# Third down pass of an encoder block: unit 8 in half-size products in three of four column groups, and the sums added to the residual in DRAM

## The chip, the cores and the metric

The kernel runs on one core of a Trainium2 chip. The core has a matrix engine (TensorE, PE in the profile), a vector engine (VectorE, DVE), a scalar engine (ScalarE, ACT), GpSimd (POOL) and SyncE (SP). Here SP only issues DMA transfers, POOL issues most of the others, and all transfers share 16 DMA engines. The metric is the device time of one execution in microseconds (us). The kernel before takes 2464.06 us, the median of three runs (2463.86 to 2465.95).

## The reference

One layer of an encoder block over 512 tokens of 2048 features, in float32. Two attention mixers come first, then a channel mixer (SwiGLU) and a final RMSNorm:

```python
x = x + g1 * (merged @ w_out[l])
h2 = rms_norm(x, norm2_w[l]) * (1.0 + sc2) + sh2
ff = (jax.nn.silu(h2 @ w_ffn_gate[l]) * (h2 @ w_ffn_up[l])) @ w_ffn_down[l]
x = x + g2 * ff
return rms_norm(x, final_w)
```

The change lies in the last product, `@ w_ffn_down`, with 5632 rows summed over, and in the sum `x + g2 * ff`.

## The kernel before

Every float32 operand of a product is split into a high and a low part (`split`, L168 on ScalarE makes the high part, L170 on VectorE the low one), and each product is three matmuls (`mm3`, L188 to L190): high by high, high by low, low by high. The 5632 rows of `w_down` are 11 units of 512 rows (four k-tiles of 128). The output's 2048 columns are worked in four groups of 512, numbered `cc` = 0 to 3.

**Two ways to multiply a unit.** `plain` takes the four k-tiles, the four token tiles and the two column halves as they are: two weight loads of 128x1024 (`wsplit`, tile `raw`), two splits, and 96 matmuls of 256 columns. The other way is Strassen's with Winograd's sums: the unit's 512x512 token block and its 512x512 weight block are cut in quarters, and seven products of half the size take the place of eight. `wforms` makes the weight forms in each group: two loads, four sums (L696 to L699, tiles `ta` and `tb`), one split of 512 and three of 1024. `sforms` makes the token forms of a unit once for all groups, with four sums and four splits, into one of three `slots` (tiles `s0`, `s1`, `s2`). This unit then costs 84 matmuls. The forms of weights go through a ring of five `whl` buffers, the raw loads through one of five `raw` buffers.

**Three passes.** Pass 1 does units 0 and 1 plain. Pass 2 does units 2, 3, 4 with half-size products and unit 5 plain. Pass 3 does units 6 and 7 with half-size products and units 8 and 9 plain; its code is the loop at the end that calls `down_group` for each `cc`. Between the passes a group's sum is kept in DRAM (`accd`). Unit 10 is done last, token tile by token tile, with the final norm. In pass 3 group 0 does its plain units first (`lead`), the others last (the `tail` of `down_group`). So the order on TensorE is 8, 9, 6, 7 | 6, 7, 8, 9 | 6, 7, 8, 9 | 6, 7, 8, 9. After a unit, `down_group` calls `behind(u)`, which is `late(cc)` in this pass, and `pump()`, which lets one piece of background work (`bg`) into the program. The eight sums of a group are added into `acc` on VectorE (L1468 to L1485).

**Where things lie.** The token pairs of plain units 8 and 9 lie in `areas`, tiles `a1` and `a0`. In pass 3 the third slot `s2` is given to other things: `xr` (the residual's column group, and two factors) and `fl` (the token pairs of unit 10).

**The residual.** `x` after the first half lies in DRAM in one tensor `x2d`. In pass 3 `residual_of` loads a column group of it into `xr` (L1569) with the row of `g2` for it (L1570). When the next group has done unit 7, `gated_sum` multiplies `acc` by the factor (L1576) and adds it to the residual (L1577), both on VectorE, and stores that to `x2pd` (L1579). During group 3 `late` loads these sums back (L1557) into places that units 6 and 7 leave.

**What sets the order.** A planner orders the instructions of each engine: of those that are ready by its own times, the one that stands first in the program goes first; some parts are marked as more urgent (`tc.high_priority`) or kept in program order (`behind`, `pin`). On the chip each engine and each DMA queue then takes its instructions strictly in that order.

Of the kernel before, what the change touches and what calls it, by code (L numbers as in the profile page):

```python
# [14 lines left out]
F32 = mybir.dt.float32  # L15
# [5 lines left out]
P = 128  # L21
WARM = 12, 14
D = 2048
# [89 lines left out]
def encoder_block(ctx: ExitStack, tc, xp, xT, c, ada1_w, ada2_w, b_ada, norm1_w, w_in, q_norm_w, k_norm_w, bias,  # L113
# [1050 lines left out]

    x2_d = dram.tile([T, D], F32, name="x2d")
    mod["queue"] = nc.sync
# [18 lines left out]
    def residual(cc, g, ssq, eng, x, keep=None):  # L1185
        cs = slice(cc * 512, (cc + 1) * 512)

        def evac(i, b):
            o = io.tile([P, 512], F32, tag="io", name="ro")
            V.tensor_mul(o, b, g[:, cs])  # L1190
            eng.tensor_add(x(i, cc), x(i, cc), o)
            if ssq:
                square(x(i, cc), ssq[i][:, cc:cc + 1])
            if keep is not None:
                t0 = i // 2 * 256 + i % 2
                nc.sync.dma_start(keep[t0:t0 + 255:2, cs], x(i, cc))
        return evac
# [185 lines left out]

    def sforms(j, u):

        big, low = slots[j]
        e, o = (raw_tile("ffe") for _ in range(2))
        for a, r in enumerate((e, o)):
            nc.gpsimd.dma_start(r, ff_d[u][:, a * 1024:(a + 1) * 1024])
        sa = wq.tile([P, 1024], F32, tag="ta", name="sa", bufs=2)  # L1390
        sb = wq.tile([P, 1024], F32, tag="tb", name="sb", bufs=1)
        a11, a21, a12, a22 = e[:, :512], e[:, 512:], o[:, :512], o[:, 512:]
        V.tensor_add(sa[:, :512], a21, a22)
        V.tensor_sub(sa[:, 512:], sa[:, :512], a11)
        V.tensor_sub(sb[:, :512], a11, a21)
        V.tensor_sub(sb[:, 512:], a12, sa[:, 512:])
        d = {}
        for src, t, at, n, rs in ((o, low, 0, 1024, (2, 4)), (a11, low, 2048, 512, (1,)), (sb, big, 2048, 1024, (7, 3)),
                                  (sa, big, 0, 1024, (5, 6))):
            if src is sa:  # L1400
                yield
            hl = [t[:, at + h * n:at + (h + 1) * n] for h in range(2)]
            split(*hl, src)
            for i, r in enumerate(rs):
                d[r] = tuple(h[:, i * 512:(i + 1) * 512] for h in hl)
        sx[u] = d
        yield
# [109 lines left out]
    f0 = 40  # L1517
    xr = p_e.tile([P, 3072 + 64], F32, tag="s23072", name="xr")
    xo = [xr[:, :2048].rearrange("p (i n) -> p i n", i=NT)]
    fl = p_e.tile([P, 4096 + 64], F32R, tag="s24096", name="fl")  # L1520
    wl = {}
    x2p_d = [dram.tile([P, NT, 512], F32, name=f"x2pd{cc}") for cc in range(3)]
    sq3 = [small.tile([P, 4], F32, tag=f"sq{i}", name=f"sq3{i}", bufs=1) for i in range(NT)]
# [8 lines left out]
    def late(cc):  # L1532
        def behind(u):
            if cc == 0 and u == 8:
                while bg:
                    pump()
            if cc == 1 and u > 7:
                a = u - 8
                xl_pairs.append(ff_pair(10, a, [fl[:, a * 2048 + e * 1024:a * 2048 + (e + 1) * 1024] for e in range(2)],
                                        pin=tc.keep_in_program_order))  # L1540
            if u == 7 and due:
                due.pop()()
            if cc == 3 and u == 6:
# [3 lines left out]
            if cc == 3 and u == 7:  # L1547
                x2.append(p_s.tile([P, NT, 512], F32, tag="s13072", name="xd"))
                gf = p_s.tile([P, 2, D], F32, tag="s14096", name="gf")
                wide2.extend((gf[:, 0], gf[:, 1]))  # L1550
                rows(wide2[0], g2_d)
            if cc == 3 and u == 9:
                for c in range(2):
                    us = [gated_split(k, c, *wtiles()) for k in range(0, 4, 2)]
                    wl[c] = [tuple(t[:, e * 512:(e + 1) * 512] for t in hl) for hl in us for e in range(2)]
                for c in range(3):
                    nc.gpsimd.dma_start(x2[c], x2p_d[c])  # L1557
                nc.scalar.dma_start(wide2[1], final_w.partition_broadcast(P))
# [5 lines left out]

    def factor(cc):
        return xr[:, 2048 + cc % 2 * 512:2560 + cc % 2 * 512]

    def residual_of(cc):
        nc.gpsimd.dma_start(xo[0], x2_d[:, cc * 512:(cc + 1) * 512].rearrange("(i p) d -> p i d", p=P))  # L1569
        nc.gpsimd.dma_start(factor(cc), g2_d[cc].partition_broadcast(P).rearrange("p o d -> p (o d)"))  # L1570

    def gated_sum(cc, acc):
        to = xo[0] if cc < 3 else x2[3]
        for t in range(2):
            ts = slice(2 * t, 2 * t + 2)
            behind(V.tensor_mul(acc[:, ts], acc[:, ts], factor(cc).unsqueeze(1).to_broadcast([P, 2, 512])))  # L1576
            behind(V.tensor_add(to[:, ts], xo[0][:, ts], acc[:, ts]))  # L1577
        if cc < 3:
            nc.gpsimd.dma_start(x2p_d[cc], xo[0])  # L1579
            residual_of(cc + 1)  # L1580

    residual_of(0)
    for cc in range(4):
        acc = acc_tile()
        nc.gpsimd.dma_start(acc, acc_d[cc])
        down_group(cc, (6, 7), cl, acc, late(cc), () if cc else (8, 9), late=cc > 1,
                   after_lead=cc == 1)
# [5 lines left out]
    for cc in range(2, 4):  # L1593
        wt = p_s.tile([P, 4096 + 64], F32R, tag=f"a{3 - cc}", name=f"w{cc}")
        hi, lo = (wt[:, 48 + e * 2048:48 + (e + 1) * 2048] for e in range(2))
# [79 lines left out]
```

## Time and profile before

| | us |
|---|---|
| median of three runs | 2464.06 |
| the profiled execution | 2474.1 |
| its span | 2472.3 |
| TensorE busy | 2435.4 |
| VectorE busy | 2007.5 |
| ScalarE busy | 1069.9 |

The profile is that of one execution. Its span runs from the first to the last instruction. TensorE's matmuls overlap in the records, so the distance between their starts is the measure of its pace. "Idle before, releaser" of a group says how long the engine rested before these instructions, and what ended most of that rest. A tile's name stands without its buffer's number.

### The profile page before, as it was taken

The page shows a single profiled execution, that of the slowest core. Times are in us where ns is not written, and L with a number is a line of the kernel's source. Part 1 is how long each engine was busy: PE and PEld are TensorE (multiplying, and loading weights), DVE is VectorE, ACT ScalarE, POOL GpSimd, SP SyncE. Part 2 cuts the span into 40 slices and gives each one's busy share as a digit, 9 for nine tenths or more (in the row PEclk, how much of TensorE's full clock was granted, in tenths as well). Part 3 has the DMA queues.
Part 4 walks back from the last instruction along what each step waited for, and adds up shares of the span by engine and source line. Part 5 has one row for each costly group of instructions (what it writes and reads, how often), then busy time and mean ns, then how long its engine had stood idle before and what let it go on. Part 6 is the DMA issues. An engine that isn't in the chain of part 4 may idle for free.

```text
span 2472.3 us, 42367 instructions
## 1 busy us (share of the span) xinstructions
PE 2435.4 (99%) x17327; PEld 2280.1 (92%) x17327; DVE 2007.5 (81%) x2704; ACT 1069.9 (43%) x1466; POOL 150.9 (6%) x255
## 2 busy tenths in 40 slices
PE   7999999999999999999999999999999999999998
PEld 6888888999888888888999999999999998999997
DVE  7995778999677678667899989889989885687877
ACT  5223455544344523237744444444444454433333
POOL 0100000000011111111000000000000010000010
PEclk9999999999999999999999999999999999999999
DMA  9874322455766687867444444445454466546563
GB/s 357 285 253 144 104 89 80 142 185 181 252 211 231 204 302 248 296 215 228 137 154 155 145 162 147 135 147 163 129 171 147 128 196 214 188 155 233 189 250 121
DMA packets 213730, 461.77 MB, mean 187 GB/s; under 512 B 15152, under 2 KB 59552, under 8 KB 204832
## 3 DMA queue, kind: packets, MB, share of 16 engines
q1 hardware_dynamic: 174160, 309.76, 38.4%
q0 software_dynamic: 29872, 132.73, 15.8%
q10 hardware_dynamic: 9504, 16.58, 1.9%
q8 instruction: 136, 2.23, 0.4%
q14 instruction: 58, 0.48, 0.1%
HBM read 412.84 MB, written 46.17 MB: 186 GB/s over the span
## 4 chain that ended last, share of the span: by engine, by line
PE 72%; DVE 14%; issue 6%; DMA 4%; ACT 1%; POOL 0%; DVEq 0%; POOLq 0%; ACTq 0%
PE mm L190 15%; PE mm L189 15%; PE mm L188 15%; PE S L188 6%; PE S L189 6%; PE S L190 6%; DVE whl L170 4%; PE Y L188 3%; PE Y L189 2%; PE Y L190 2%; DVE raw L524 2%; DMA raw<-in_w_down 2%; DMA raw<-in_w_up 1%; PE T L886 1%; DVE g_acc L631 1%
## 5 line engine op out<-in xcount | busy, mean ns | idle before, releaser
L168 ACT ACTIVATE whl<-raw 128x1024 fp32r<-128x1024 f32 (+1 forms) x483 | 453.9, 943 | 671.1 <-PE mm L190 288.4
L170 DVE TENSOR_TENSOR whl<-raw,whl 128x1024 fp32r<-128x1024 f32 (+1 forms) x483 | 517.9, 1087 | 126.3 <-ACT whl L168 125.9
L168 ACT ACTIVATE whl<-ta 128x1024 fp32r<-128x1024 f32 x124 | 131.4, 1059 | 181.8 <-PE mm L190 107.6
L168 ACT ACTIVATE whl<-tb 128x1024 fp32r<-128x1024 f32 x124 | 131.4, 1060 | 174.5 <-PE S L190 109.8
L170 DVE TENSOR_TENSOR whl<-ta,whl 128x1024 fp32r<-128x1024 f32 x124 | 151.2, 1220 | 40.7 <-ACT whl L168 40.1
L388 DVE SCALAR_TENSOR_TENSOR acc<-mw,cact,acc 128x1024 f32<-128x1024 f32 x124 | 158.8, 1281 | 18.3 <-DMA mw<-in_ada_w 17.9
L170 DVE TENSOR_TENSOR whl<-tb,whl 128x1024 fp32r<-128x1024 f32 x124 | 150.9, 1217 | 4.6 <-ACT whl L168 4.5
L366 POOL DMA_DIRECT2D mw<-in_ada_w x113 | 60.3, 534 | 1361.5 <-DVE acc L388 946.5
L697 DVE TENSOR_TENSOR ta<-raw,ta 128x512 f32<-128x512 f32 x124 | 85.2, 687 | 69.3 <-DMA raw<-in_w_down 29.7
L696 DVE TENSOR_TENSOR ta<-raw 128x512 f32<-128x512 f32 x124 | 85.3, 688 | 36.7 <-DMA raw<-in_w_down 34.3
L188 PE MATMUL mm<-x56h,whl 128*128 128x256 f32 x336 | 92.5, 275 | 0.4 <-DVE c L784 0.4
L189 PE MATMUL mm<-x56l,whl 128*128 128x256 f32 x336 | 92.4, 275 | 0.0
L190 PE MATMUL mm<-x56h,whl 128*128 128x256 f32 x336 | 92.4, 275 | 0.0
L189 PE MATMUL mm<-whl,s 128*128 128x256 f32 x320 | 88.2, 276 | 1.0 <-DVE whl L170 0.8
L188 PE MATMUL mm<-x3h,whl 128*128 128x256 f32 x320 | 88.1, 275 | 0.0
L188 PE MATMUL mm<-whl,s 128*128 128x256 f32 x320 | 88.1, 275 | 0.0
L189 PE MATMUL mm<-x3l,whl 128*128 128x256 f32 x320 | 88.0, 275 | 0.0
L190 PE MATMUL mm<-x3h,whl 128*128 128x256 f32 x320 | 88.0, 275 | 0.0
L188 PE MATMUL S<-x56h,whl 128*128 128x256 f32 x320 | 88.0, 275 | 0.0
L189 PE MATMUL S<-x56l,whl 128*128 128x256 f32 x320 | 88.0, 275 | 0.0
L190 PE MATMUL S<-x56h,whl 128*128 128x256 f32 x320 | 88.0, 275 | 0.0
L190 PE MATMUL mm<-whl,s 128*128 128x256 f32 x320 | 88.0, 275 | 0.0
(1879 smaller groups left out, 8910.9 us busy)
## 6 DMA issues: line engine op xcount, KB each, us to landing
raw<-in_w_in SPq DMA_DIRECT2D x133, 512.0 KB, 4.6
mw<-in_ada_w POOLq DMA_DIRECT2D x113, 512.0 KB, 4.5
raw<-in_w_gate SPq DMA_DIRECT2D x92, 512.0 KB, 4.6
raw<-in_w_up SPq DMA_DIRECT2D x88, 512.0 KB, 4.6
raw<-in_w_down SPq DMA_DIRECT2D x88, 512.0 KB, 5.4
raw<-in_ada_w POOLq DMA_DIRECT2D x29, 1024.0 KB, 6.6
raw<-in_w_out SPq DMA_DIRECT2D x48, 512.0 KB, 5.5
ffd<-c SPq DMA_DIRECT2D x10, 1024.0 KB, 4.8
```

The lines of the kernel that those rows point to most:

```text
L168: high = pin(S.activation(hi, src, AF.Copy))
L170: latest[:] = [high, pin(eng.tensor_sub(lo, src, hi))]
L188: nc.tensor.matmul(o, lh, rh, start=start, stop=False, **kw)
L189: nc.tensor.matmul(o, lh, rl, start=False, stop=False, **kw)
L190: nc.tensor.matmul(o, ll, rh, start=False, stop=stop, **kw)
L366: mod["queue"].dma_start(w, ada2_w[n * P:(n + 1) * P, :])
L388: behind(V.scalar_tensor_tensor(acc, part, cact[:, k:k + 1], acc, op0=ALU.mult, op1=ALU.add))
L524: V.scalar_tensor_tensor(raw, raw, 1.0, call, op0=ALU.mult, op1=ALU.mult, accum_out=y)
L631: V.tensor_add(acc, acc, b)
L696: V.tensor_sub(t1, b12, b11)
L697: V.tensor_sub(t2_, b22, t1)
L886: nc.tensor.transpose(tp[:, k * P:(k + 1) * P], e[:, k * P:(k + 1) * P], ident)
```

## The change

Unit 8 is plain in group 0 alone. In groups 1, 2 and 3 it is done in half-size products after units 6 and 7, and unit 9 stays plain. The order on TensorE becomes 8, 9, 6, 7 | 6, 7, 8, 9 | 6, 7, 8, 9 | 6, 7, 8, 9, with unit 8 of 84 matmuls behind each bar.

The token forms of unit 8 go into slot `s2`. They are made in group 0 behind units 6 and 7, as background work. Their input and sums have a place of their own, the tile `a1` that unit 8's plain pairs leave (`room`): one load of 1 MB on SP's queue, in place of two `raw` buffers and the `ta` and `tb` buffers.

Since `s2` is taken, `xr` is no more. The gated sum of groups 0 to 2 is added to the residual in DRAM by a transfer that adds (`accum_op`), two for a group, issued on POOL's queue; VectorE's two additions for each of these groups are left out. To that end `x2d` becomes eight tensors, one for each column group and token half. Group 3's residual is loaded into SBUF and added there as before. The factors get two small tiles. The token pairs of unit 10 (`fl`) go to `a1` behind the forms, and are loaded on SP's queue. The last weights of group 2 go to `s2` rather than `a1`.

```diff
-    x2_d = dram.tile([T, D], F32, name="x2d")
+    x2_d = [[dram.tile([256, 512], F32, name=f"x2d{cc}{t}") for t in range(2)] for cc in range(4)]
...
-                t0 = i // 2 * 256 + i % 2
-                nc.sync.dma_start(keep[t0:t0 + 255:2, cs], x(i, cc))
+                nc.sync.dma_start(keep[cc][i // 2][i % 2::2, :], x(i, cc))
...
-    def sforms(j, u):
+    def sforms(j, u, room=None):
...
+        else:
+            e, o, sa, sb = (room[:, n * 1024:(n + 1) * 1024] for n in range(4))
+            nc.sync.dma_start(room[:, :2048], ff_d[u])
+            yield
...
+    x2_of = lambda cc, t: x2_d[cc][t].rearrange("(i p) d -> p i d", p=P)
+
+    def load_x2(to, cc):
+        for t in range(2):
+            nc.gpsimd.dma_start(to[:, 2 * t:2 * t + 2], x2_of(cc, t))
...
+            if cc == 0 and u == 9:
+                forms = sforms(2, 8, p_s.tile([P, 4096 + 64], F32, tag="a1", name="f8"))
+                next(forms)
+                bg.append(forms)
             if cc == 1 and u > 7:
                 a = u - 8
-                xl_pairs.append(ff_pair(10, a, [fl[:, a * 2048 + e * 1024:a * 2048 + (e + 1) * 1024] for e in range(2)],
-                                        pin=tc.keep_in_program_order))
-            if u == 7 and due:
-                due.pop()()
+                if a == 0:
+                    fl.append(p_s.tile([P, 4096 + 64], F32R, tag="a1", name="fl"))
+                xl_pairs.append(ff_pair(10, a, [fl[0][:, a * 2048 + e * 1024:a * 2048 + (e + 1) * 1024] for e in range(2)],
+                                        nc.sync, pin=tc.keep_in_program_order))
...
                 rows(wide2[0], g2_d)
+                load_x2(x2[3], 3)
+            if u == 7 and due:
+                due.pop()()
...
                 for c in range(3):
-                    nc.gpsimd.dma_start(x2[c], x2p_d[c])
+                    load_x2(x2[c], c)
...
-    def residual_of(cc):
-        nc.gpsimd.dma_start(xo[0], x2_d[:, cc * 512:(cc + 1) * 512].rearrange("(i p) d -> p i d", p=P))
-        nc.gpsimd.dma_start(factor(cc), g2_d[cc].partition_broadcast(P).rearrange("p o d -> p (o d)"))
+    def factor_of(cc):
+        f = p_e.tile([P, 512], F32, tag="g2f", name="g2f", bufs=2)
+        nc.gpsimd.dma_start(f, g2_d[cc].partition_broadcast(P).rearrange("p o d -> p (o d)"))
+        factors.append(f)

     def gated_sum(cc, acc):
-        to = xo[0] if cc < 3 else x2[3]
+        f = factors.pop(0).unsqueeze(1).to_broadcast([P, 2, 512])
         for t in range(2):
             ts = slice(2 * t, 2 * t + 2)
-            behind(V.tensor_mul(acc[:, ts], acc[:, ts], factor(cc).unsqueeze(1).to_broadcast([P, 2, 512])))
-            behind(V.tensor_add(to[:, ts], xo[0][:, ts], acc[:, ts]))
+            behind(V.tensor_mul(acc[:, ts], acc[:, ts], f))
+            if cc == 3:
+                behind(V.tensor_add(x2[3][:, ts], x2[3][:, ts], acc[:, ts]))
+            else:
+                nc.gpsimd.dma_start(x2_of(cc, t), acc[:, ts], accum_op=ALU.add)
         if cc < 3:
-            nc.gpsimd.dma_start(x2p_d[cc], xo[0])
-            residual_of(cc + 1)
+            factor_of(cc + 1)
...
-        down_group(cc, (6, 7), cl, acc, late(cc), () if cc else (8, 9), late=cc > 1,
+        down_group(cc, (6, 7, 8) if cc else (6, 7), {9: cl[9]} if cc else cl, acc, late(cc), () if cc else (8, 9), late=cc > 1,
                    after_lead=cc == 1)
...
-        wt = p_s.tile([P, 4096 + 64], F32R, tag=f"a{3 - cc}", name=f"w{cc}")
+        wt = (p_e if cc == 2 else p_s).tile([P, 4096 + 64], F32R, tag="s24096" if cc == 2 else "a0", name=f"w{cc}")
```

More of the change, by code (lines that the diff above doesn't have):

```diff
@@ L1382, in __getitem__ @@
             return tuple(Tokens(half(t)[:, :, q]) for t in self.pairs[j])
-    def sforms(j, u):
+    def sforms(j, u, room=None):
         big, low = slots[j]
[L1387 to L1391, printed above, removed]
+        if room is None:
+            e, o = (raw_tile("ffe") for _ in range(2))
+            for a, r in enumerate((e, o)):
+                nc.gpsimd.dma_start(r, ff_d[u][:, a * 1024:(a + 1) * 1024])
+            sa = wq.tile([P, 1024], F32, tag="ta", name="sa", bufs=2)
+            sb = wq.tile([P, 1024], F32, tag="tb", name="sb", bufs=1)
+        else:
+            e, o, sa, sb = (room[:, n * 1024:(n + 1) * 1024] for n in range(4))
+            nc.sync.dma_start(room[:, :2048], ff_d[u])
+            yield
         a11, a21, a12, a22 = e[:, :512], e[:, 512:], o[:, :512], o[:, 512:]
@@ L1517, in encoder_block @@
     f0 = 40
[L1518 to L1522, printed above, removed]
+    fl, wl = [], {}
+    x2_of = lambda cc, t: x2_d[cc][t].rearrange("(i p) d -> p i d", p=P)
+    def load_x2(to, cc):
+        for t in range(2):
+            nc.gpsimd.dma_start(to[:, 2 * t:2 * t + 2], x2_of(cc, t))
     sq3 = [small.tile([P, 4], F32, tag=f"sq{i}", name=f"sq3{i}", bufs=1) for i in range(NT)]
@@ L1563, in encoder_block @@
     due = []
-    def factor(cc):
-        return xr[:, 2048 + cc % 2 * 512:2560 + cc % 2 * 512]
-    def residual_of(cc):
-        nc.gpsimd.dma_start(xo[0], x2_d[:, cc * 512:(cc + 1) * 512].rearrange("(i p) d -> p i d", p=P))
-        nc.gpsimd.dma_start(factor(cc), g2_d[cc].partition_broadcast(P).rearrange("p o d -> p (o d)"))
+    def factor_of(cc):
+        f = p_e.tile([P, 512], F32, tag="g2f", name="g2f", bufs=2)
+        nc.gpsimd.dma_start(f, g2_d[cc].partition_broadcast(P).rearrange("p o d -> p (o d)"))
+        factors.append(f)
     def gated_sum(cc, acc):
-        to = xo[0] if cc < 3 else x2[3]
+        f = factors.pop(0).unsqueeze(1).to_broadcast([P, 2, 512])
         for t in range(2):
             ts = slice(2 * t, 2 * t + 2)
-            behind(V.tensor_mul(acc[:, ts], acc[:, ts], factor(cc).unsqueeze(1).to_broadcast([P, 2, 512])))
-            behind(V.tensor_add(to[:, ts], xo[0][:, ts], acc[:, ts]))
+            behind(V.tensor_mul(acc[:, ts], acc[:, ts], f))
[3 more added lines that the diff above has]
+                nc.gpsimd.dma_start(x2_of(cc, t), acc[:, ts], accum_op=ALU.add)
         if cc < 3:
-            nc.gpsimd.dma_start(x2p_d[cc], xo[0])
-            residual_of(cc + 1)
-    residual_of(0)
+            factor_of(cc + 1)
+    factors = []
+    factor_of(0)
     for cc in range(4):
```

## The prediction

> **What bounds the kernel now.** I read the page first, for the engine that fills the span.
>
> ```profile
> span 2472.3 us, 42367 instructions
> PE 2435.4 (99%) x17327; PEld 2280.1 (92%) x17327; DVE 2007.5 (81%) x2704; ACT 1069.9 (43%) x1466; POOL 150.9 (6%) x255
> ```
>
> TensorE is busy 99% of the span, VectorE is second. The change sits in the third down pass, so next I read busy time in that pass's four column groups (columns: stretch, length, then busy time and count of PE, PEld, DVE, ACT, POOL, the clock, DMA share, GB/s).
>
> ```profile
> 2258.10:2298.30 40.20, 40.20 (x362) 40.20 (x361) 30.82 (x40) 15.82 (x17) 1.61 (x3) 1.00 0.60 202
> 2298.30:2338.50 40.20, 40.20 (x362) 40.20 (x361) 35.39 (x44) 14.34 (x15) 2.91 (x5) 1.00 0.59 204
> 2338.50:2378.70 40.20, 40.20 (x362) 40.20 (x361) 30.96 (x39) 12.44 (x13) 2.39 (x4) 1.00 0.56 200
> 2378.70:2418.90 40.20, 40.20 (x362) 40.20 (x361) 28.84 (x30) 13.65 (x14) 5.03 (x9) 1.00 0.80 294
> ```
>
> TensorE never rests in these 160.8 us and holds full clock. A group is 360 matmuls by the code (two half-size units of 84, two plain units of 96), so a matmul takes 40.20/360 = 0.1117 us. VectorE is the next limit, 35.4 of 40.2 us in the second group. All that TensorE waits for from 2240 us to the end:
>
> ```profile
> PE S L189 <- DVE whl L170: 1.0, 1, 1.0
> PE mm L189 <- DVE w L170: 0.3, 1, 0.3
> ```
>
> So every matmul removed is worth its full 0.1117 us, as long as VectorE delivers the forms in time. To see how much time it has, I place the units on TensorE's timeline.
>
> ```profile
> 2279.54 0.28 PE L188 MATMUL mm<-whl,s 128*128 128x256 f32 x1
> ...
> 2317.06 0.28 PE L188 MATMUL Y<-whl,a 128*128 128x256 f32 x1
> ...
> 2418.90 0.38 PE L188 MATMUL S<-whl,fl 128*128 128x512 f32 x1
> ```
>
> Group 0's plain units 8 and 9 end at 2279.54, so unit 8 ends 96 × 0.1117 earlier, at 2268.82. Four half-size units follow without a break (6 and 7 of group 0, 6 and 7 of group 1), 9.38 us each, until 2317.06. The last product of group 3 ends at 2418.90.
>
> **The matmuls removed.** A plain unit is 4 k-tiles × 4 token tiles × 2 halves × 3 terms = 96 matmuls; a half-size one is 7 products × 2 × 2 × 3 = 84. Groups 1, 2 and 3 lose 12 each: 36 × 0.1117 = **4.02 us**, the whole gain on the bounding engine, and less than 0.2% of the run (4.93 us), which is about what a measurement of this kernel can tell from no change.
>
> **VectorE's price.** Its queue in the stretch with four units in a row:
>
> ```profile
> 2273.10 0.69 DVE L696 TENSOR_TENSOR ta<-raw 128x512 f32<-128x512 f32 x1 [6.18 <-DMA raw<-in_w_down]
> ...
> 2274.91 0.69 DVE L170 TENSOR_TENSOR whl<-raw,whl 128x512 fp32r<-128x512 f32 x1
> ...
> 2284.25 1.82 DVE L170 TENSOR_TENSOR whl<-raw,whl 128x512 fp32r<-128x512 f32 x2
> ...
> 2289.11 0.69 DVE L697 TENSOR_TENSOR ta<-raw,ta 128x512 f32<-128x512 f32 x1 [1.18 <-DMA raw<-in_w_down]
> ...
> 2301.65 1.21 DVE L170 TENSOR_TENSOR whl<-tb,whl 128x1024 fp32r<-128x1024 f32 x1
> ...
> 2303.39 0.68 DVE L698 TENSOR_TENSOR tb<-raw 128x512 f32<-128x512 f32 x1
> 2303.99 0.68 DVE L699 TENSOR_TENSOR tb<-raw,ta 128x512 f32<-128x512 f32 x1
> 2304.59 1.21 DVE L170 TENSOR_TENSOR whl<-raw,whl 128x1024 fp32r<-128x1024 f32 x1
> 2305.73 1.21 DVE L170 TENSOR_TENSOR whl<-ta,whl 128x1024 fp32r<-128x1024 f32 x1
> 2306.86 1.21 DVE L170 TENSOR_TENSOR whl<-tb,whl 128x1024 fp32r<-128x1024 f32 x1
> 2308.00 1.21 DVE L1576 TENSOR_TENSOR acc<-acc,xr 128x1024 f32<-128x1024 f32 x1
> ```
>
> From start to start, a 512-wide operation takes 0.60 us and a 1024-wide one 1.14. A unit's weight forms are four sums, one short split and three long ones: 4 × 0.60 + 0.60 + 3 × 1.14 = 6.42 us; a plain unit's two splits are 2.28. So each of groups 1 to 3 gains 4.14 us of VectorE work. The token forms of unit 8, made once in group 0, have the same operations: 6.42 us. Against that the three residual sums of groups 0 to 2 go, six of these:
>
> ```profile
> L1577 DVE TENSOR_TENSOR xr<-xr,acc 128x1024 f32<-128x1024 f32 x6 | 7.3, 1222 | 0.1
> ```
>
> Six × 1.14 = 6.84 us. The balance is 3 × 4.14 + 6.42 − 6.84 = +12.0 us. The pass then has 126.0 + 12.0 = 138 us of VectorE work in 156.8 us: it fits on average. Groups 2 and 3 I cost at nothing; what hides them is VectorE's own idle time there (9 and 11 us of each 40.2), against 4.14 − 2.28 = +1.9 us each. ScalarE gains a split and a half per unit and is busy 12 to 16 us of 40.
>
> Groups 0 to 1 are another matter. From 2273.10 to 2308 VectorE rests only 1.18 us, and into this stretch goes all of the 6.42 us: the token forms' load needs the place that unit 8 leaves at 2268.82, and their work is given out behind units 6 and 7 of group 0, ahead of the forms of unit 7 and of group 1. How late are the forms then? Unit 7's first, at 2284.25 + 0.60, is needed at 2279.54 + 9.38 = 2288.92: slack 4.1. The last one of group 1's unit 6 is done at 2301.65 + 1.21 = 2302.86 and needed 60 matmuls after 2298.30, at 2305.00: **slack 2.14 us**, the tightest point I find. After it the slack grows: unit 7's last form is done at 2308.07 and needed 60 matmuls after 2307.68, at 2314.38, 6.3 us later. So 6.42 us put in ahead of the tightest point make TensorE wait 6.42 − 2.14 = **4.28 us**. Then unit 8 of group 1: VectorE reaches it at 2308.0 + 6.42 + 2 × 1.14 (the two products of group 0's sum that stay) = 2316.7, needs 6.42 and is done at 2323.1; TensorE wants the last form at 2317.06 + 4.28 + 6.70 = 2328.0. No second wait.
>
> The bounds of this wait: 0, if the work slips into time that I count as full; 4.28 − 1.14 − 1.18 = 1.96, if the fourth split falls behind the tight point and the one idle gap is used; and above, what a wait costs beyond itself. The only other wait of the down passes shows that, in the second pass's last group, where token forms were also made beside three half-size units:
>
> ```profile
> 2231.30 0.28 PE L190 MATMUL S<-whl,s 128*128 128x256 f32 x1
> 2232.44 0.38 PE L188 MATMUL S<-whl,s 128*128 128x256 f32 x1 [0.87 <-ACT whl L168]
> 2233.70 0.38 PE L189 MATMUL S<-whl,s 128*128 128x256 f32 x1 [0.88 <-DVE whl L170]
> ```
> ```profile
> 2229.00:2240.00 11.00, 9.25 (x66) 8.87 (x65) 9.98 (x13) 6.01 (x7) 1.58 (x3) 0.84 0.82 287
> ```
>
> Two waits, 2.2 us beyond the normal pace, and then a mean clock of 0.84 over 11 us: 0.16 × 11 = 1.76 us more. I take 4.28 and keep 0 and 4.28 + 1.76 = 6.04 for the range. The Trainium skill, "TensorE: Matmul & The Clock Gate", Part 1, says the clock falls only after about 3.4 us of idling; by it the sequel would not come from waits this short, and the upper end would be 4.28. The row speaks against it, and the row decides.
>
> **The other edits.** Ten 1 MB transfers of the residual become six half-size sums in DRAM and eight half-size loads, plus one 1 MB load of unit 8:
>
> ```profile
> xr<-x2d POOLq DMA_DIRECT2D x4, 1024.0 KB, 10.3
> x2pd<-xr POOLq DMA_DIRECT2D x3, 1024.0 KB, 5.2
> xa<-x2pd POOLq DMA_DIRECT2D x2, 1024.0 KB, 7.4
> xb<-x2pd POOLq DMA_DIRECT2D x1, 1024.0 KB, 9.5
> ```
>
> No row shows a transfer that adds; I bound it by a plain store, 5.2 us, and twice the slowest row, 20.6. Group 2's sum is issued about 2390 and its columns are read after 2418.90: even 20.6 + 10.3 us of transfer and reload are nearly covered, so 0, nearest to the store. On POOL's queue the reloads, and the next group's accumulator load, stand behind the sums; the accumulator is wanted again only a group later, after 40 us. The token pairs of unit 10 move from POOL's queue to SP's, the last weights of group 2 into another tile, the factors into two small ones: covered the same way, 0 each (a lost cover would cost at most one landing, 5 to 10 us). In the last stretch,
>
> ```profile
> 2405.22 1.23 DVE L1528 TENSOR_TENSOR raw<-raw,gf 128x1024 f32<-128x1024 f32 x1 [3.25 <-DMA gf<-g2d]
> ```
>
> the gate row arrives 2405.22, freed by unit 7 of group 3. The end of the pass comes 1.34 us sooner after that unit than before, so between −1.3 us (its present waits gone) and +1.34 (as much later). I take 0.
>
> **Sum:** −4.02 + 4.28 = +0.26 us on the profiled execution's 2474.1 (span 2472.3 and 1.8 around it), 2474.4. That execution is 10.0 us over the median of the runs; the difference carries over unchanged: 2464.06 + 0.26 = **2464.3**.
>
> **Rivals.** *The forms are hidden* (no wait): for it, form making elsewhere runs beside full TensorE, and the order on VectorE is a planner's, which may put them elsewhere; against it, the stretch is full. −4.02, with up to 1.34 given back at the end: 2460.0 to 2461.4, middle 2460.7; with the last stretch's waits gone too, 2458.7.
>
> *SP's queue stands* (slower). The load of unit 8 is given out on SP ahead of unit 6's weights and waits for TensorE until 2268.82. Before, SP issued weights at these times:
>
> ```profile
> 2263.42 0.37 SPq L195 DMA_DIRECT2D raw<-in_w_down  x1
> 2266.95 0.37 SPq L195 DMA_DIRECT2D raw<-in_w_down  x1
> ```
>
> If it stands ahead of them, the second goes out at 2269.2, 2.3 us later, behind 1 MB (2.8 us, an estimate: group 3's 294 GB/s at a share of 0.80 make 368 GB/s in full). Queued behind it are all later weights, and VectorE waits for them: it starts 5.1 us later than 2273.10, and the tightest point is 4.28 + 5.1 = 9.4 us late: −4.02 + 9.4 + 1.76 = +7.1, 2471.2. With that sequel it is slower by over 0.2% from 2.9 us of delay upward. Against it: the planner may give the weights out first, as they are ready 1.9 us sooner.
>
> *The change does not get its third group*: unit 8 of group 1 is fed too late and only two groups gain, 2 × 1.34 less the same wait: 2464.06 − 2.68 + 4.28 = 2465.7. The 4.9 us of slack worked out above speak against it.
>
> **Chances.** The wait eats the gain 0.42 (2462.0 to 2466.1), hidden 0.27, SP stands 0.18, third group 0.05, the rest (order elsewhere, the end) 0.08. Faster by over 0.2% needs the hidden case and the last waits gone: 0.10, with 0.03 of the rest, 0.13. Slower: SP 0.18 and 0.04: 0.22. Within: 0.65. The range reaches from just under 2458.7 to just over 2471.2.
>
> **What would show it.** Right: 252 matmuls on forms in groups 1 to 3; VectorE without rest from 2273 to 2323; one or more TensorE waits on forms between 2288 and 2306, about 4 us together; nothing from then to the end of group 3. Hidden: no wait there and 28.1 us per three units in each group. SP: the load of unit 8 issued before the two weights, and VectorE's first sum after 2277. Wrong altogether: a wait that is not on VectorE's forms, or a last stretch over 2 us longer or shorter.

## The result and the profile after

The changed kernel takes 2492.45 us (median of four runs, 2490.23 to 2495.96) against 2465.01 us for the kernel before beside it: 1.0107 times as long, with a 95% interval from 1.0095 to 1.0119. That is 27.4 us slower (23 to 29). The prediction said 2464.3 us with a range to just over 2471.2, so it failed, and with it every rival that it had priced.

The page of the changed kernel begins (busy time, share and count of each engine):

```profile
span 2489.2 us, 42338 instructions
PE 2433.5 (98%) x17291; PEld 2277.1 (91%) x17291; DVE 2018.4 (81%) x2724; ACT 1077.5 (43%) x1476; POOL 157.0 (6%) x257
```

TensorE has 36 matmuls less, and VectorE has 10.9 us more, about the 12.0 that were worked out. So the changed work is what was foreseen, and the time lies in waits. All waits of TensorE from 2240 us on (waiter, releaser, us in total, times, longest):

```profile
PE Y L189 <- DVE whl L170: 11.2, 1, 11.2
PE mm L189 <- DVE whl L170: 2.9, 3, 1.8
PE mm L188 <- ACT w L168: 2.8, 1, 2.8
PE S L189 <- DVE whl L170: 2.8, 3, 1.7
PE Y L188 <- DVE acc L1489: 1.9, 1, 1.9
PE mm L189 <- DVE w L170: 1.8, 1, 1.8
PE T L189 <- DVE whl L170: 1.5, 1, 1.5
```

Before there were two, 1.3 us in all. To place them, the pass is cut at the first matmul of each run of units. These are busy times by stretch (same columns as in the prediction): the five half-size units of groups 0 and 1; group 1's unit 9; group 2's half-size units and its unit 9; the same two for group 3; unit 10 as the last stretch.

```profile
2270.89:2323.47 52.58, 47.96 (x423) 47.20 (x421) 45.52 (x57) 25.15 (x28) 3.07 (x3) 1.00 0.46 124
2323.47:2334.19 10.72, 10.72 (x99) 10.72 (x97) 9.77 (x14) 3.08 (x3) 0.57 (x1) 1.00 0.90 329
2334.19:2364.11 29.92, 28.93 (x254) 28.36 (x253) 22.97 (x30) 11.84 (x13) 3.05 (x3) 1.00 0.53 133
2364.11:2375.09 10.98, 10.98 (x98) 10.79 (x97) 6.48 (x10) 2.13 (x2) 0.58 (x1) 1.00 0.65 240
2375.09:2405.39 30.30, 28.41 (x254) 28.21 (x253) 20.74 (x26) 10.18 (x11) 3.91 (x4) 1.00 0.67 189
2405.39:2429.02 23.63, 12.42 (x98) 12.23 (x97) 11.47 (x14) 4.01 (x4) 6.49 (x10) 0.78 0.73 248
2429.02:2479.53 50.51, 44.13 (x206) 37.59 (x204) 43.19 (x71) 16.09 (x39) 0.00 (x0) 0.97 0.24 84
```

Before, the last stretch read:

```profile
2418.90:2462.48 43.58, 42.23 (x206) 36.51 (x204) 38.50 (x67) 15.13 (x37) 0.00 (x0) 1.00 0.23 83
```

At full pace 420 half-size matmuls take 46.9 us, 252 take 28.14 and 96 take 10.72. So groups 0 and 1 lose 5.7 us, group 2 loses 1.8 + 0.3, group 3's half-size units 2.2, its unit 9 12.9, and the last stretch 6.9 over before. Together that is 29.8, less the 4.0 of the matmuls: 25.8 us, within the interval of the measured difference. The two spans differ by 16.9 us only, since the profiled execution of before was itself 10 us over its median: its group 0 begins unit 6 at 2279.54, 8.65 us later than here, so most of that lies ahead of these stretches. Stage by stage the two can be compared.

The largest loss begins on POOL's queue in group 3. After:

```profile
2387.23 0.72 POOL L1527 DMA_DIRECT2D xa<-x2d  x1 [22.50 <-PE mm L190]
2389.80 1.22 POOL L1591 DMA_DIRECT2D x2d<-acc  x1 [1.86 <-DVE acc L1587]
2396.93 1.22 POOL L1591 DMA_DIRECT2D x2d<-acc  x1 [5.91 <-issue]
2397.66 1.25 POOL L1527 DMA_DIRECT2D xa<-x2d  x1
2405.57 1.46 POOL L1527 DMA_DIRECT2D xa<-x2d  x2 [6.67 <-issue]
2407.01 1.65 POOL L439 DMA_DIRECT2D gf<-g2d  x3
```

Before:

```profile
2396.69 1.60 POOL L439 DMA_DIRECT2D gf<-g2d  x3 [2.52 <-PE S L190]
```

The first load of the gate row (`gf`, L439) goes out 2407.01 − 2375.09 = 31.9 us after group 3's start; before it was 2396.69 − 2378.70 = 18.0 us. Ahead of it stand the two adding transfers and the reloads, and POOL stands 5.91 and 6.67 us for which the view names no releaser. The landing times in the trace do: the two adding transfers landed at 2396.61 and 2405.26 (6.8 and 8.3 us after they went out), and each time POOL went on 0.3 us later, at 2396.93 and 2405.57. So POOL stood each time until the adding transfer before had landed. What waits for the row is VectorE:

```profile
2394.68 1.23 DVE L170 TENSOR_TENSOR whl<-tb,whl 128x1024 fp32r<-128x1024 f32 x1
2413.86 1.23 DVE L1534 TENSOR_TENSOR raw<-raw,gf 128x1024 f32<-128x1024 f32 x1 [17.95 <-DMA gf<-g2d]
2415.00 0.68 DVE L1475 TENSOR_TENSOR acc<-acc,p 128x512 f32<-128x512 f32 x1
2415.60 2.35 DVE L170 TENSOR_TENSOR whl<-raw,whl 128x1024 fp32r<-128x1024 f32 x2
```

The product of the last unit's weights with the gate row stands in VectorE's order ahead of group 3's sums (L1475) and of the splits for group 3's unit 9 (L170, 2415.60). VectorE rests 17.95 us with all of them behind it, and TensorE waits 11.2 us for those splits. The wait carries the name of VectorE's `whl`, but its cause is a transfer on a queue of another engine.

### The profile page after: what moved, and what is told of

It reads as the page before. It is cut to its first block, busy times and chain, and to the rows that moved or that the text cites. A ratio compares the mean times of both kernels' runs of the same rounds, so it can differ in the third digit from the quotient of the medians.

```text
span 2489.2 us, 42338 instructions
## 1 busy us (share of the span) xinstructions
PE 2433.5 (98%) x17291; PEld 2277.1 (91%) x17291; DVE 2018.4 (81%) x2724; ACT 1077.5 (43%) x1476; POOL 157.0 (6%) x257
## 4 chain that ended last, share of the span: by engine, by line
PE 70%; DVE 15%; DMA 6%; issue 5%; ACT 1%; POOL 0%; DVEq 0%; SPq 0%; POOLq 0%; ACTq 0%
PE mm L190 15%; PE mm L189 15%; PE mm L188 15%; PE S L188 6%; PE S L190 5%; PE S L189 5%; DVE whl L170 4%; DMA raw<-in_w_down 4%; PE Y L188 2%; PE Y L189 2%; PE Y L190 2%; DVE raw L524 2%; PE T L886 1%; DMA ffr<-ffd 1%; DVE acc L1489 1%
## 5 line engine op out<-in xcount | busy, mean ns | idle before, releaser
L170 DVE TENSOR_TENSOR whl<-raw,whl 128x1024 fp32r<-128x1024 f32 (+1 forms) x483 | 515.8, 1083 | 121.8 <-ACT whl L168 121.5
L170 DVE TENSOR_TENSOR whl<-ta,whl 128x1024 fp32r<-128x1024 f32 x127 | 154.8, 1219 | 41.8 <-ACT whl L168 41.8
L170 DVE TENSOR_TENSOR whl<-tb,whl 128x1024 fp32r<-128x1024 f32 x127 | 154.5, 1217 | 3.3 <-ACT whl L168 3.1
L189 PE MATMUL mm<-whl,s 128*128 128x256 f32 x368 | 101.6, 276 | 3.0 <-DVE whl L170 2.9
L188 PE MATMUL mm<-whl,s 128*128 128x256 f32 x368 | 101.3, 275 | 0.0
L190 PE MATMUL mm<-whl,s 128*128 128x256 f32 x368 | 101.2, 275 | 0.0
```

The lines of the kernel that those rows point to most:

```text
L170: latest[:] = [high, pin(eng.tensor_sub(lo, src, hi))]
L188: nc.tensor.matmul(o, lh, rh, start=start, stop=False, **kw)
L189: nc.tensor.matmul(o, lh, rl, start=False, stop=False, **kw)
L190: nc.tensor.matmul(o, ll, rh, start=False, stop=stop, **kw)
```

## The experiments

Each kernel was timed beside the kernel before, and ratios are to that.

**1. The gate row on another queue.**

```diff
-    def rows(dst, src):
+    def rows(dst, src, queue=nc.gpsimd):
...
-                rows(wide2[0], g2_d)
+                rows(wide2[0], g2_d, nc.scalar)
```

> The changed kernel with one edit: the four loads of the gate row for the last stretch are issued on ScalarE's queue instead of POOL's. Theory A (the gate row is late because it stands on POOL's queue behind the adding transfers and the reloads, and VectorE, which waits 17.9 us for it in order, keeps unit 9's weight splits and the sums of group 3 behind it): the row goes out near 2394 instead of 2407, the 11.2 us wait of TensorE in unit 9 of group 3 goes, and most of the 6.9 us by which the last stretch is longer; 2492.5 - 13 to 20 = 2473 to 2480. Rival B (the adding transfers crowd the DMA engines, so that whatever loads then is late): the row lands 7 us or more after its issue plus the delay it has now, less than 3 us gained, 2489 to 2492. Rival C (the half-size unit 8 overloads VectorE, the wait for the row is only where that shows): no gain, 2490 to 2493.

Measured: 2476.41 us, ratio 1.0043 (1.0028 to 1.0059), 16 us less than the change (1.0107 to 1.0043 of 2465 us). In its trace the row goes out 19.7 us after group 3's start (2393.23, group 3 from 2373.57), VectorE's rest for it shrinks to 4.46 us, and group 3's unit 9 runs at full pace:

```profile
2393.23 2.13 ACTq L439 DMA_DIRECT2D gf<-g2d  x4
2398.74 2.36 DVE L1534 TENSOR_TENSOR raw<-raw,gf 128x1024 f32<-128x1024 f32 x2 [4.46 <-DMA gf<-g2d]
```

So the queue behind which the row stood is shown as the largest cause. ScalarE's queue does not owe this to a faster transfer: counted from group 3's start the row's first part landed 13.7 us sooner than in the change, 12.3 of them since it went out sooner and 1.4 since it took 5.4 us from issue to landing in place of 6.8. In the stages, 12.9 of the 16 us are those that group 3's unit 9 lost. The waits in groups 0 and 1, the 1.8 us in group 3 and a last stretch of 50.7 us stay.

**2. Plain stores in place of adding ones.** The products of groups 0 to 2 are stored plainly into tensors of their own and reloaded from there; the residual of these groups is left out.

```diff
-                nc.gpsimd.dma_start(x2_of(cc, t), acc[:, ts], accum_op=ALU.add)
+                nc.gpsimd.dma_start(x2s_of(cc, t), acc[:, ts])
...
```

> The changed kernel, but the six adding transfers are plain stores of the gated product to DRAM tensors of the same shape, and the reloads read these (so the residual of groups 0 to 2 is left out of the sum). Theory A, if POOL's standing of 5 to 7 us after each adding transfer is a property of adding: the second of a pair and all behind it go out some 6 us earlier, the gate row lands 6 to 9 us earlier, 2492.5 - 6 to 9 = 2483 to 2487. If the standing comes from the number of descriptors on POOL's queue, which is the same here: no change, 2490 to 2493. Rival B: most of the 20 us come back, 2472 to 2478. Rival C: no change.

Measured: 2485.62 us, ratio 1.008 (1.0062 to 1.0097), 6.7 us less than the change.

```profile
2392.23 0.73 POOL L1595 DMA_DIRECT2D x2s<-acc  x1 [0.88 <-DVE acc L1591]
2393.38 0.71 POOL L1595 DMA_DIRECT2D x2s<-acc  x1 [0.41 <-DVE acc L1591]
...
2400.22 0.55 POOL L439 DMA_DIRECT2D gf<-g2d  x1
```

A plain store holds POOL 0.72 us, an adding one 1.22, and after a plain one POOL goes on within 0.8 us in place of about 6. The gate row leaves 19.6 us after group 3's start (2380.64), but POOL stands here too, 2.2 to 3.3 us three times among the reloads and the parts of the row. The row's last part is issued as late as 2407.79, and TensorE still waits 3.5 us before unit 9.

**3. Unit 8 plain, the sums in DRAM kept.**

```diff
-        down_group(cc, (6, 7, 8) if cc else (6, 7), {9: cl[9]} if cc else cl, acc, ...
+        down_group(cc, (6, 7), cl, acc, ...
...
```

> The changed kernel with unit 8 plain in all four groups, as before, and no token forms of it; sums into DRAM, factors, reloads and their queues stay. Theory A: TensorE gets 4.0 us of matmuls more, the 5.7 us of waits in groups 0 and 1 go, and the last part stays late, since the gate row still stands behind the sums and reloads: 2492.5 + 4.0 - 5.7 - 0 to 6 = 2485 to 2491. Rival C: the time of the kernel before comes back, 2463 to 2467. Rival B: 2488 to 2491.

Measured: 2484.97 us, ratio 1.0075 (1.0057 to 1.0093). Without any change to the products the kernel is still 18 us slower. All four groups are at full pace; the row leaves at 2409.20 and the loss of this pass lies in the last stretch (from 2418.99), whose first 24 matmuls take 18.4 us, with these waits:

```profile
PE S L189 <- DVE whl L170: 9.6, 4, 5.4
```

The stretch takes 56.1 us against 43.6 before. That is 12.6 of the 18 us; the rest is not placed, since this profiled execution, like that of before, was already late when group 0 began unit 6 (2279.63).

**4. The token forms put off by one step of the background work.**

```diff
-                bg.append(forms)
+                bg.append(itertools.chain([None], forms))
```

> The changed kernel with the token forms of unit 8 given out one unit later: their sums and three splits behind unit 7 of group 0 instead of unit 6, the last split behind unit 6 of group 1. The theory of the record (VectorE's 6.42 us of forms are too much in groups 0 and 1, wherever they stand): the waits there stay at 4 to 6 us, 2490 to 2494. The other reading of the new trace (VectorE stands 5.3 us in order for the load of unit 8, with unit 6's last weight form behind it; the work itself would nearly fit): the waits in groups 0 and 1 fall from 5.7 to 1 to 3 us, 2487 to 2491. The last part stays late by either.

Measured: 2491.88 us, ratio 1.0104 (1.0082 to 1.0126). The planner gave out the forms at nearly the same place (groups 0 and 1 take 52.2 us in place of 52.6), so the edit did not do what it was meant to, and it tells nothing of the forms. The next two hold them back by a dependency instead, and both have the gate row on ScalarE's queue.

**5. The forms held behind group 0's unit 7.** Their sums and splits may go out only after the last weight form of that unit.

```diff
-                bg.append(forms)
+                bg.append(itertools.chain([None] * 1, forms))
...
+        held = [] if room is None else latest[:]
+        with tc.issue_after(held[1].ins) if held else contextlib.nullcontext():
             V.tensor_add(sa[:, :512], a21, a22)
...
+            hold[:] = held
             split(*hl, src)
+            hold.clear()
...
```

> The gate row on ScalarE's queue (as in the run before, 2476.4), and the token forms of unit 8 held, on VectorE and ScalarE, behind the last weight form of group 0's unit 7. They still stand ahead of the tightest point of the record (the last form of group 1's unit 6), but nothing urgent stands behind VectorE's wait for their load any more. The theory of the record (6.42 us of work against 2.14 us of slack): 4.3 us of waits in groups 0 and 1, against 6.4 in the run before, 2474 to 2475. The reading that VectorE's standing for the load makes the wait: 0 to 1.5 us of waits, 2470 to 2472.

Measured: 2475.77 us, ratio 1.0038 (1.0024 to 1.0051). In the change VectorE rests 5.33 us for the forms' load with unit 6's last weight form behind it:

```profile
2275.15 0.69 DVE L1397 TENSOR_TENSOR f<-f 128x512 f32<-128x512 f32 x1 [5.33 <-DMA f<-ffd]
...
2278.10 1.22 DVE L170 TENSOR_TENSOR whl<-tb,whl 128x1024 fp32r<-128x1024 f32 x1
```

Here that rest is gone, and yet groups 0 and 1 take 52.31 us, 5.4 over full pace; the four waits have become one, at the start of group 1's unit 6:

```profile
PE mm L189 <- DVE whl L170: 3.5, 1, 3.5
```

Behind that wait the granted clock reads 0.50 (2296.00 to 2299.30); 3.4 us at half clock are another 1.7 us, so that wait and clock make 5.2 of the 5.4. So the rest for the load is not the cause by itself: the forms are 6.4 us of work ahead of a point that leaves less than that.

**6. The forms held behind group 1's unit 6.** The same with `[None] * 2`.

> As the one with the forms behind unit 7 of group 0, but held behind the last weight form of group 1's unit 6, which is the tightest point: all of the work then comes after it, where the record finds 6.3 us of slack growing. By the record: 0 to 2.7 us of waits (the forms of unit 8's weights come late by that if the gated products go first), 2470 to 2473. If it is the mere amount of VectorE work between 2262 and 2317 that counts, wherever it stands: 4 us or more, 2474 to 2476.

Measured: 2472.23 us (ten runs), ratio 1.0029 (1.0017 to 1.0041). Groups 0 and 1, then groups 1 (unit 9) and 2, then group 3, then the last stretch:

```profile
2271.52:2320.02 48.50, 47.60 (x422) 47.12 (x421) 46.41 (x59) 24.24 (x27) 3.07 (x3) 1.00 0.51 139
2320.02:2369.60 49.58, 49.58 (x446) 49.58 (x445) 42.14 (x56) 17.25 (x18) 4.19 (x5) 1.00 0.67 206
2369.60:2408.46 38.86, 38.86 (x350) 38.86 (x349) 33.10 (x38) 14.47 (x15) 6.97 (x9) 1.00 0.83 263
2408.46:2458.13 49.67, 43.92 (x206) 37.47 (x204) 38.73 (x67) 16.25 (x38) 1.24 (x2) 0.97 0.31 113
```

The tight point is passed, groups 2 and 3 have no wait at all (38.86 us is 28.14 + 10.72), and 1.6 us are left in groups 0 and 1, where VectorE is busy 46.41 of 48.50 us: this is what the added work costs when its place is good. The 1.8 to 1.9 us wait in group 3 went too, though nothing there was changed; why is not settled. The last stretch is still 49.67. Its longest wait, with what leads to it:

```profile
2421.61 1.22 DVE L1538 TENSOR_TENSOR raw<-raw,gf 128x1024 f32<-128x1024 f32 x1
2422.86 1.06 ACT L168 ACTIVATE w<-raw 128x1024 fp32r<-128x1024 f32 x1 [6.95 <-DVE raw L1538]
2423.97 0.80 PE L188 MATMUL mm<-w,fl 128*128 128x512 f32 x1 [3.15 <-ACT w L168]
```

TensorE waits for ScalarE's split, and that for a gate product on VectorE, which works without rest from 2411.26 until then, on group 3's sums among other things.

**7. The gate row taken out of the weights altogether.** Experiment 1, and all columns are multiplied by the row when they are taken from PSUM, where the matmuls leave their sums; before, only column group 2 was.

```diff
-        if cc != 2:
+        if False:
             V.tensor_mul(r3, r3, wide2[0]...
...
-        if cc == 2:
+        if True:
             g = io.tile(...
```

> The gate row on ScalarE's queue, and the weights of the last unit are not multiplied by the gate row beforehand (six 1024-wide products of VectorE); instead every column's sum is multiplied when it is taken from PSUM, as group 2's already is (12 more 512-wide products, spread over the last stretch). What is left of the loss at the end (7.1 us of waits on the weights of the last unit, after the gate row comes in time). If VectorE's pile causes it (sums of group 3, splits and products all after the gate row, 30 us of work from 2398 on): 6.8 us less of it, 4 to 6 us gained, 2470 to 2472. If the full DMA engines cause it (share 1.0 from 2390 to 2420): the weights come no sooner, 0 to 1.5 us, 2475 to 2477.

Measured: 2479.74 us, ratio 1.0059 (1.0036 to 1.0082), not the 2470 to 2472 that the theory gave. Last stretch on TensorE, and what follows its last matmuls:

```profile
2415.18:2457.77 42.59, 42.23 (x206) 36.43 (x204) 38.78 (x69) 15.20 (x34) 2.15 (x3) 1.00 0.33 115
2457.77:2473.80 16.03, 0.00 (x0) 0.00 (x0) 10.06 (x26) 3.39 (x10) 0.00 (x0) 0.65 0.37 131
```

TensorE's waits in the last stretch are gone but for 0.3 us, so it was VectorE's pile of work (sums of group 3, gate products, splits) that held it. With the products went VectorE's rest for the row, 4.46 us in experiment 1; the two were not separated here, but experiment 10 keeps that rest. But VectorE now ends late: 10.06 us of its work in 16.03 us stand behind the last matmul; in the change the same tail is 9.67 us. The work was moved to a worse place.

**8. Unit 8 plain and the gate row on ScalarE's queue** (the edits of 1 and 3).

> Unit 8 plain in all groups, sums into DRAM as in the change, gate row on ScalarE's queue. If the 7.1 us at the end and the waits in groups 0 to 3 come from the half-size unit 8 (its forms, and a tail of one plain unit where there were two, to hide group 3's VectorE work under): the time of the kernel before, 2463 to 2467. If the adding transfers and reloads by themselves cost something besides the gate row (full DMA engines): 2469 to 2473.

Measured: 2466.39 us, ratio 1.0006 (0.9996 to 1.0017): the time of before. From group 0's unit 6 to the end of group 3, and the last stretch:

```profile
2274.02:2413.38 139.36, 139.36 (x1251) 139.36 (x1249) 108.42 (x130) 49.71 (x52) 14.08 (x16) 1.00 0.63 193
2413.38:2455.08 41.70, 41.69 (x206) 36.67 (x204) 34.78 (x63) 14.13 (x36) 1.42 (x2) 1.00 0.33 115
```

Adding in DRAM costs nothing that can be told from noise once nothing urgent stands behind it on the queue: here too the second adding transfer of group 2 goes out 8.3 us after the first (2383.99 and 2392.28), and TensorE waits for nothing from 2240 us on. All that is left in experiment 1 comes with the half-size unit 8. With the change and experiments 1 and 3 this makes a square: taking the row off POOL's queue gains 0.64% with unit 8 half-size and 0.69% with it plain, so the two losses stand beside each other.

**9. A tail of two plain units in group 3 again.** Experiment 6, but group 3 does unit 8 plain, its token pairs loaded and split anew into `s2`.

```diff
-        down_group(cc, (6, 7, 8) if cc else (6, 7), {9: cl[9]} if cc else cl, acc, ...
+        down_group(cc, (6, 7, 8) if cc in (1, 2) else (6, 7),
+                   {8: again, 9: cl[9]} if cc == 3 else {9: cl[9]} if cc else cl, acc, ...
...
+            if cc == 2 and u == 8:
+                f8 = p_e.tile([P, 4096 + 64], F32R, tag="s24096", name="f8p")
+                for a in range(2):
+                    again[a] = ff_pair(8, a, [f8[:, a * 2048 + e * 1024:a * 2048 + (e + 1) * 1024] for e in range(2)],
+                                       nc.sync, pin=tc.keep_in_program_order)
...
```

> The forms held back and the gate row on ScalarE's queue as in the last run of that kind (2472.2 us), and now unit 8 is half-size in groups 1 and 2 only. In group 3 it is plain again, with its token pairs loaded and split anew into slot s2 during group 3. Group 3 so gets back the 12 matmuls (+1.34 us) and a tail of two plain units, 21.44 us on TensorE in place of 10.72. Theory A (the last stretch is late because a tail of one unit is too short to hide the end-of-group sums, the splits and the gate products): the last stretch falls from 49.7 us to 42 to 44.5, and the time is 2472.2 + 1.3 - (5.2 to 7.7) = 2465.8 to 2468.3. Theory B (it is late for another reason that stays, such as late reloads or the late gate row): the last stretch stays at 48 to 51, and the time is 2472 to 2476. Theory C (the anew loaded token pairs, 2 MB more, get in the way of group 3's weights): waits on forms in group 3 itself, over 2474.

Measured: 2470.04 us, ratio 1.0013 (1.0003 to 1.0022). The last stretch falls from 49.67 to 45.77 us, between the two theories:

```profile
2411.93:2457.70 45.77, 43.61 (x206) 37.84 (x204) 37.30 (x65) 14.25 (x36) 2.15 (x3) 0.96 0.38 134
```

VectorE is no longer late by its work; it rests for weights that arrive late:

```profile
2415.94 1.23 DVE L1538 TENSOR_TENSOR raw<-raw,gf 128x1024 f32<-128x1024 f32 x1 [2.87 <-DMA raw<-in_w_down]
```

So the longer tail does help, by 3.9 us here. What is left over experiment 8's 41.70 is one wait of 2.16 us behind this rest and a low clock after it (last section). The weights may be late because of the 2 MB that this experiment loads anew, which was not tested. A plain unit 8 also needs 4.14 us less of VectorE's time for its weights in group 3, by the prediction's count, so length of tail and amount of work were not separated.

**10. Two column groups multiplied afterwards.** Experiment 6, with the gate row multiplied into the weights of column groups 0 and 1 alone.

```diff
-        if cc != 2:
+        if cc < 2:
             V.tensor_mul(r3, r3, wide2[0]...
...
-        if cc == 2:
+        if cc > 1:
             g = io.tile(...
```

> Forms held back and gate row on ScalarE's queue (2472.2 us), unit 8 half-size in all three groups, and the gate row is multiplied into the weights only for columns groups 0 and 1; columns 2 and 3 are multiplied when taken from PSUM (before: column 2 only). This takes 2 x 1.14 = 2.3 us of VectorE's work out of the pile before the last stretch and puts about 4 x 0.6 us into the last stretch. Theory A (VectorE's pile is the bound of the last stretch): the waits there shrink by 2.3 to 4 us, the last stretch is 45.5 to 47.5 in place of 49.7, the time 2468 to 2470.5. Theory B (ScalarE's splits, held by late weights, are the bound): unchanged within 1.5 us, 2471 to 2473.5.

Measured: 2468.02 us (ten runs) beside 2466.32, ratio 1.0000 (0.9989 to 1.0011).

```profile
2408.72:2452.46 43.74, 42.42 (x206) 36.54 (x204) 37.07 (x66) 15.99 (x36) 1.16 (x2) 1.00 0.36 131
2452.46:2464.10 11.64, 0.00 (x0) 0.00 (x0) 6.00 (x19) 2.67 (x8) 0.00 (x0) 0.72 0.26 90
```

Taking 2.3 us of VectorE's work away ahead of the last stretch shortens it by 5.9 us, 49.67 to 43.74, more than the 4 expected: TensorE's waits there fall from 5.8 to 1.4 us, and 3.4 us at half clock behind them, worth 1.7, do not come. The change now costs nothing, and it brings nothing. The gain of 4.0 us is eaten by 1.6 us in groups 0 and 1, 0.4 in group 3, 0.2 in the last stretch and 1.8 in a tail of 11.64 us against 9.82 before (from the last matmuls at 2462.48 to 2472.3).

**11. More room for descriptors.** The change as it is, and `dynamic_dma_scratch_size` 1472 in place of 1024.

> The change as it is, with dynamic_dma_scratch_size 1472 in place of 1024: more room for the descriptors that POOL writes. Theory A (POOL stands 5 to 6 us after an adding transfer since the room for descriptors is full): at least one of the two long rests in group 3 falls below 2 us, the gate row is issued 3 to 10 us sooner than at 2407.0, and the time falls by 3 to 10 us, 2482 to 2489. Theory B (the rest belongs to the adding transfer itself): rests of 5 to 7 us as before, gate row within 1.5 us, the time 2490 to 2494.

Measured: 2496.05 us, ratio 1.0116 (1.0098 to 1.0133), no faster. But POOL's queue in group 3 reads:

```profile
2394.25 0.72 POOL L1527 DMA_DIRECT2D xa<-x2d  x1 [26.44 <-PE mm L190]
2395.14 2.45 POOL L1591 DMA_DIRECT2D x2d<-acc  x2 [0.17 <-issue]
...
2406.90 2.15 POOL L439 DMA_DIRECT2D gf<-g2d  x4 [3.25 <-ACT whl L168]
```

The two adding transfers go out back to back, 0.17 us after what stood ahead, in place of 5.91 us apart; the pairs of groups 0 and 1 close up in the same way. The landing times say how POOL stands. With 1024, the second adding transfer of a pair goes out 0.3 us after the first has landed, in all 30 pairs of the ten runs that have them. In this pass a plain transfer that has to stand goes out 0.3 us after the landing of the one three to five issues ahead; the kernel before did so too in group 3, four issues behind:

```profile
2405.51 0.54 POOL L439 DMA_DIRECT2D gf<-g2d  x1 [2.19 <-issue]
```

With 1472 the plain ones stand for the landing of the one six or seven ahead, or three or four where adding ones are among them. So the setting bounds how much POOL may have under way, and an adding transfer takes up more of that than a plain one; the addition as such does not make POOL stand. That this is room for descriptors is what the setting is read as; no view shows it. The gate row now leaves 22.6 us after group 3's start (2384.30) in place of 31.9, and the wait before unit 9 falls from 11.2 to 4.9 us. Group 3 itself starts 9.2 us later, though, 8.1 of it lost from group 0's unit 6 to the end of group 2, since VectorE rests longer for weights in groups 1 and 2, among other places here:

```profile
2367.40 0.69 DVE L697 TENSOR_TENSOR ta<-raw,ta 128x512 f32<-128x512 f32 x1 [6.24 <-DMA raw<-in_w_down]
```

Whether that is the denser traffic, or the planner's order, which came out different in places, was not separated.

**The steps in one row.** The change 1.0107; gate row on another queue 1.0043; forms held back 1.0029; two column groups afterwards 1.0000. In us of 2465: +26.4, +10.6, +7.1, 0. The intervals of 1.0043 and 1.0029 overlap, so the step between these two is shown by its trace and not by its time. The profiled executions of experiments 6, 7 and 10 were 2.9, 4.1 and 2.2 us under the medians of their runs, so their stages are to be compared with stages only. No version beats the kernel before: even without its remaining losses this one could gain 4.0 us, 0.16%.

## Why the prediction was wrong

**The matmuls removed: right.** 36 fewer, and groups 2 and 3 take 28.14 + 10.72 = 38.86 us each in experiment 6, against 40.20 before.

**VectorE's price in groups 0 and 1: right in size, not in the point.** The text put 6.42 us ahead of a slack of 2.14 and took 4.28 us, at most 6.04. Measured were 5.7 us, 4.6 of them in four waits (1.5 on `T`, then 1.8, 0.7 and 0.6). Only the last, 0.6 us, is at the point that was named, the last form of group 1's unit 6. The others are in units 6 and 7 of group 0, since the forms, and VectorE's rest of 5.33 us for their load, went ahead of unit 6's last form as well; the text had counted no such rest. That the size still came near is in part luck. Experiments 5 and 6 show the tight point at work: held behind unit 7 the forms cost 5.4 us, held behind group 1's unit 6 they cost 1.6. The sequel of a wait, 1.76 us, that the text kept for its upper end came in these groups in experiment 5 and not in the change.

**SP's queue stands: did not happen.** The load went out at 2266.35, behind the two weights that it was feared to hold up; the next weights went out at 2284.10, long after it had landed. VectorE's rest at 2275.15 is for this load itself.

**The other edits: this step failed.** It said that "On POOL's queue the reloads, and the next group's accumulator load, stand behind the sums", and costed them at 0. It asked how late the sums and the accumulator would be, which are wanted late. It did not ask for everything else on that queue: the gate row's load comes behind them too, VectorE already rested 3.25 us for it before (the row at 2405.22 in the prediction), so it had no slack, and VectorE meets it ahead of group 3's sums and unit 9's splits. The price was 16 us (experiment 1). The bounds that were given for the landing of an adding transfer, 5.2 to 20.6 us, held: 6.5 us in the median, 6.8 and 8.3 for group 2's two. But the text let only the readers of the sums wait for it, "even 20.6 + 10.3 us of transfer and reload are nearly covered, so 0". POOL itself stood until each had landed, and with it all of its queue. Before, POOL stood in this way too, but for plain transfers only, 2.19 and 1.01 us in group 3.

**The last stretch: this step failed too.** "between −1.3 us (its present waits gone) and +1.34 (as much later). I take 0." looked only at the gate row's arrival. Measured were +6.9 us, and it remains (50.7 us) when the gate row leaves early. With unit 8 half-size, the tail behind the last half-size unit is 10.72 us long and no longer 21.44, and into it fall group 3's sums, the gate products and the splits of the last weights. Experiments 7, 9 and 10 bear this out: work taken away (42.59 and 43.74 us) and a longer tail, with less work (45.77), each shorten it.

**VectorE in groups 2 and 3 at nothing: nearly right.** As changed, they lost 2.1 and 2.2 us. With the forms held back and the row early they lose nothing.

**The range** had its bounds from the four terms named, so an omitted reader of a shared queue was outside it. The text did name the sign: "a wait that is not on VectorE's forms, or a last stretch over 2 us longer" would make it wrong altogether. The first came in disguise, since the trace writes the 11.2 us wait to VectorE's `whl`; only the row ahead of it in VectorE's order tells that a transfer was the cause.

## What to carry to other kernels

When work moves onto a DMA queue, list everything issued on that queue behind it until the end of the stage, and for each transfer the engine that waits for it and what stands behind that waiter; price the first late one, not the ones that were moved. Ask also how long the moved transfer keeps the issuing engine: here until it had landed. A unit made faster also takes away cover: if a faster product leaves a shorter tail, ask what was hidden under it. Work moved off a pile must not land behind the last matmul (experiment 7); a third of it moved gained more over its own base (experiment 10).

## What the runs showed of the hardware

An adding transfer of 512 KB holds POOL 1.22 us, a plain one 0.72. With `dynamic_dma_scratch_size` at 1024 POOL then stands 4.7 to 7.1 us before the second of a pair, until 0.3 us after the first has landed; with 1472 the second follows the first without a rest. The Trainium skill, "DMA: Bandwidth & Descriptors", section "Issuing engines are not separate DMA queues", says that issuing from several engines saves only the time to initiate transfers, usually small beside the transfer itself. In experiment 1 the gain is of that kind, since the same row was only issued from another engine, but it is not small: 16 us, against 5.4 to 6.8 us that a part of the row takes to land. What was saved was the standing of the queue.

A short wait can cost more than itself. In experiment 9 TensorE waits once for 2.16 us early in the last stretch, until 2418.35, and then (two stretches of 2 us):

```profile
2418.00:2420.00 2.00, 1.65 (x4) 1.38 (x5) 2.00 (x4) 0.26 (x1) 0.00 (x0) 0.58 0.90 342
2420.00:2422.00 2.00, 2.00 (x7) 1.61 (x6) 2.00 (x4) 0.00 (x0) 0.00 (x0) 0.57 0.30 113
```

The granted clock is 0.58 and 0.57 there, 1.00 before and after. The Trainium skill, "TensorE: Matmul & The Clock Gate", Part 1, gives about 3.4 us of idling as what lets the clock fall; this row has it after 2.2 us. In experiments 1 to 6 the last stretch pays this sequel as well. A wait of this size need not bring it: behind the wait of 1.8 us in group 0's unit 7 the clock reads 1.00 in the change (2285.00 to 2288.50) and 0.52 in experiment 1 (the same times). What decides between the two is not shown.
